# Sample attention with a plain f32 product, the two maps combined in one VectorE step, and the merge's panels split on ScalarE and VectorE

## The chip, the core and the metric

The kernel runs on one core of a Trainium2 chip. The core has TensorE (matrix products, PE in the profile, with PEld for the loading of its stationary operand), VectorE (DVE), ScalarE (ACT), GpSimd (POOL) and SyncE (SP, which here issues all DMA transfers). Each engine works through its own instructions in a fixed order; semaphores hold an instruction until what it needs is there. The metric is the time of one execution on the device in microseconds (us), as the median of several runs.

## The reference, cut to what matters

One layer of an encoder is applied to two sequences, a prompt of 512 tokens and a sample of 1024, each of width 1024. The part that the change touches is the attention, whose map is the difference of two softmax maps:

```python
def block(args):                                  # 128 queries at a time, 8 heads
    s = jnp.einsum('bqhmd,bkhmd->bhmqk', qblk, kf) * scale      # m: the two maps
    p = jax.nn.softmax(s + bias[None, :, None], axis=-1)
    a = p[:, :, 0] - lam * p[:, :, 1]
    return jnp.einsum('bhqk,bkhe->bqhe', a, vf)   # value width 128
...
g = jax.nn.sigmoid(gates)
merged = g[:, :, 0] * (att @ w_proj_attn) + g[:, :, 1] * (y_ssm @ w_proj_ssm)
return merged @ w_out
```

Before it stand an RMS norm and a large input projection, beside it a state-space branch (y_ssm), behind it a norm with a residual and a gated feed-forward network. All data are f32.

## The kernel before

Tiles have 128 partitions. For precision, nearly every product is made of three matmuls in the type f32r: an operand x is split into a high part (x rounded to f32r) and a low part (x minus the high part), and `gemm` (L162 to L167) adds high x high, high x low and low x high in one PSUM tile. `split` (L133) makes the two parts: "act_dve" with a ScalarE copy (L136) and a VectorE subtraction (L137), otherwise with two GpSimd steps (L142, L143). `split_panel` (L145) does this for a panel of 256 weight columns in two halves of 128 x 1024.

The stages, in the order of time: input norm; projections, with the prompt's attention laid between those of keys and queries; convolution, state-space scans and gates; then the sample's attention together with "side work" (32 blocks of gated products with 24 matmuls of 512 columns each: one pass of w_proj_attn for the prompt, three passes of w_proj_ssm); then the merge stage; then the feed-forward network.

The attention goes head by head (8), and in a head over query tiles of 128, in pairs (q2). For a query tile and each of the two maps it makes the scores (s, L291 and L292: four matmuls of 512 columns for 1024 keys), adds the bias and finds the minimum on VectorE (L294), and takes the exponential on ScalarE (L297). Then the maps are combined: VectorE does the first half of the keys in one step (L304), GpSimd the other half in two (L303, L306); VSH = 4 sets the halves. The combined map is transposed on TensorE in blocks of 128 (t, L310); ScalarE copies four blocks as the high part (L313) and VectorE makes the low part (L314). For a pair of query tiles the product with the values (o, out of `gemm`) takes three matmuls of 256 columns for each block of 128 keys. The values' two parts (vh, vl) are made on GpSimd. At the end of 512 queries a mean square (ms, L328) is made for the later norm.

The merge stage runs on 512-token chunks: `load_merged` for the prompt, then `out_proj` (panels of w_out, products of 256 columns), `merge` for each of the two sample chunks (panels of w_proj_attn, products of 512 columns, gated on VectorE), and `norms` (L1054 to L1077: norm, residual, second norm, transposes). The panels of `out_proj` and `merge` are split on GpSimd before the change.

The order of the instructions on each engine is set when the program is built: a scheduler of the framework simulates the program with costs of its own and lets each engine take what is ready, with the order of the code as the priority. So a change of what an engine has to do also changes where other instructions stand.

Of the kernel before, what the change touches and what calls it, by code (L numbers as in the profile page):

```python
# [18 lines left out]
P = 128  # L19
# [10 lines left out]
Q0, K0, V0, Z0, XBC0, DT0, G0 = 0, 1024, 2048, 3072, 4096, 5632, 5664  # L30
SEGK = 119
SKP = 2304
VSH = 4
PU = (1, 1)
OT = ("gt", 2)
NG = 2
# [42 lines left out]
def hybrid_trunk_kernel(ctx: ExitStack, tc: tile.TileContext, a: dict, y_prompt, y_sample):  # L79
# [48 lines left out]
    def staged(pool, shape, *srcs, tag="raw", bufs=None):  # L128
        raw = pool.tile(shape, F32, tag=tag, name=tag, bufs=bufs)
        for part, src in srcs:  # L130
            load(out=raw[part] if part is not None else raw, in_=src)
        return raw

    def split(hi, lo, raw, eng=None):
        if eng == "act_dve":
            S.copy(hi, raw)  # L136
            V.tensor_sub(lo, raw, f(hi))  # L137
        elif eng == "act_pool":
            S.copy(hi, raw)
            G.tensor_sub(lo, raw, f(hi))  # L140
        else:
            G.tensor_scalar(hi, raw, 1.0, 0.0, op0=ALU.mult, op1=ALU.add)  # L142
            G.tensor_sub(lo, raw, f(hi))  # L143
# [18 lines left out]
    def gemm(ps, pairs):  # L162
        n = len(pairs)
        for i, (ah, al, bh, bl) in enumerate(pairs):
            TE.matmul(ps, ah, bh, start=(i == 0), stop=False)  # L165
            TE.matmul(ps, ah, bl, start=False, stop=False)  # L166
            TE.matmul(ps, al, bh, start=False, stop=(i == n - 1))  # L167
# [96 lines left out]
    def attention(base, SL, h, got, pend, zq, msq, qk, pp, at, qr, s_ps, t_ps, o_ps):  # L264
        nkb = SL // P
        tb = got["tb"]
        qh, ql, km = zip(got[0], got[1])
        v_h = at.tile([P, nkb, P], F32R, tag="vh", name="vh", bufs=1)
        v_l = at.tile([P, nkb, P], F32R, tag="vl", name="vl", bufs=1)
        raw = staged(qr, [P, nkb, P], (None, v_d[base:base + SL, h * P:(h + 1) * P].rearrange("(b p) e -> p b e", p=P)))  # L270
        split(v_h[:], v_l[:], raw[:])
        for qc in range(SL // 512):
            ops = o_ps.tile([P, 512], F32, tag="o", name="o")
            for q2 in range(2):
                aT = [at.tile([P, 2, 4, 256], F32R, tag=f"aT{b0}", name="aT", bufs=2 - b0 // 4)
                      for b0 in range(0, nkb, 4)]
                for u in range(2):
                    if pend and (q2, u) == PU:
                        pend.pop()()
                    qt = qc * 4 + q2 * 2 + u  # L280
                    qs = slice(qt * P, (qt + 1) * P)
                    off = P * (nkb - 1 - qt)
                    nm = pp.tile([P, 2], F32, tag="nm", name="nm")
                    zs = pp.tile([P, 2], F32, tag="zs", name="zs")
                    z0 = zq[:, h, qt:qt + 1]
                    pm = []
                    for m in range(2):
                        sps = s_ps.tile([P, SL], F32, tag="s", name="s")
                        for kc in range(0, SL, 512):
                            ks = slice(kc, kc + 512)  # L290
                            TE.matmul(sps[:, ks], qh[m][:, qs], km[m][:, ks], start=True, stop=False)  # L291
                            TE.matmul(sps[:, ks], ql[m][:, qs], km[m][:, ks], start=False, stop=True)  # L292
                        pt = pp.tile([P, SL], F32, tag=f"p{m}", name="pt", bufs=3)
                        V.tensor_tensor_reduce(out=pt[:], in0=sps[:], in1=tb[:, off:off + SL], scale=-1.0,  # L294
                                               scalar=3.0e38, op0=ALU.add, op1=ALU.min,
                                               accum_out=nm[:, m:m + 1])
                        S.activation(out=pt, in_=pt, func=AF.Exp, bias=nm[:, m:m + 1], scale=-1.0,  # L297
                                     accum_out=(z0, zs[:, 0:1])[m])
                        pm.append(pt)
                    V.reciprocal(zs[:, 0:1], zs[:, 0:1])  # L300
                    V.scalar_tensor_tensor(zs[:, 1:2], zs[:, 0:1], z0, neglam, op0=ALU.mult, op1=ALU.mult)  # L301
                    ca, cb = slice(0, SL * VSH // 8), slice(SL * VSH // 8, SL)
                    G.tensor_scalar(pm[1][:, cb], pm[1][:, cb], zs[:, 1:2], 0.0, op0=ALU.mult, op1=ALU.add)  # L303
                    V.scalar_tensor_tensor(pm[0][:, ca], pm[1][:, ca], zs[:, 1:2], pm[0][:, ca],  # L304
                                           op0=ALU.mult, op1=ALU.add)
                    last_add.append(G.tensor_add(pm[0][:, cb], pm[0][:, cb], pm[1][:, cb]))  # L306
                    for b0 in range(0, nkb, 4):
                        ps = t_ps.tile([P, 4, P], F32, tag="t", name="t")
                        for j in range(4):
                            TE.transpose(ps[:, j, :], pm[0][:, (b0 + j) * P:(b0 + j + 1) * P], ident)  # L310
                        us = slice(u * P, (u + 1) * P)
                        ab = aT[b0 // 4]
                        S.copy(ab[:, 0, :, us], ps)  # L313
                        V.tensor_sub(ab[:, 1, :, us], ps, f(ab[:, 0, :, us]))  # L314
                    if u == 0:
                        yield
                gemm(ops[:, q2 * 256:q2 * 256 + 256],
                     [(v_h[:, b, :], v_l[:, b, :], aT[b // 4][:, 0, b % 4, :], aT[b // 4][:, 1, b % 4, :]) for b in range(nkb)])
                yield
            av = pp.tile([P, 512], F32, tag="av", name="av", bufs=1)  # L320
            S.copy(av, ops)
            store(out=att_d[h * P:(h + 1) * P, base + qc * 512:base + qc * 512 + 512], in_=av)

            def mean_square(av=av, qc=qc):
                S.activation(out=av, in_=av, func=AF.Square)
                ps = t_ps.tile([P, 4, P], F32, tag="t", name="ms")
                for j in range(4):
                    TE.matmul(ps[:, 0, j:j + 1], av[:, j * P:(j + 1) * P], onec, start=True, stop=True)  # L328
                V.tensor_copy(msq[:, h, qc * 4:qc * 4 + 4], ps[:, 0, 0:4])
            pend.append(mean_square)  # L330
# [538 lines left out]
    with ExitStack() as ph3:  # L869
# [22 lines left out]
        def merge(c, aTt):  # L892
            cs = slice(c * 512, (c + 1) * 512)
            hi, lo = big_pair()
            for p0 in range(0, D, 256):
                w = split_panel(a["w_proj_attn"][0][:, p0:p0 + 256], eng="pool")
                for b in range(2):
                    r0 = p0 + b * P
                    kb = r0 // P
                    gt = wk.tile([P, 512], F32, tag="gt", name="gt")  # L900
                    pt = wk.tile([P, 512], F32, tag="pt", name="pt", bufs=1)
                    load(out=gt, in_=g_d[r0:r0 + P, cs])
                    S.activation(out=gt, in_=gt, func=AF.Tanh, scale=0.5)
                    load(out=pt, in_=part_d[r0:r0 + P, cs])
                    ps = mm_tile(512)
                    gemm_fm(ps, w, slice(b * P, (b + 1) * P), aTt)
                    V.scalar_tensor_tensor(gt, gt, 1.0, ps, op0=ALU.add, op1=ALU.mult)
                    V.tensor_add(gt, gt, pt)
                    S.activation(out=hi[:, kb, :], in_=gt, func=AF.Copy, scale=0.5)
                    V.scalar_tensor_tensor(lo[:, kb, :], gt, 0.5, f(hi[:, kb, :]), op0=ALU.mult, op1=ALU.subtract)  # L910
            return hi, lo
# [120 lines left out]
        with ExitStack() as ph3a:  # L1032
# [4 lines left out]
            def out_proj(mT):  # L1037
                tiles = [mp.tile([P, D], F32, tag="mt", name="mt", bufs=4) for _ in range(4)]
                sums = wk.tile([P, 4, 4], F32, tag="ms4", name="ms4")
                for p0 in range(0, D, 256):  # L1040
                    w = split_panel(a["w_out"][0][:, p0:p0 + 256], eng="pool")
                    for j in range(4):
                        ps = mm_tile(256)
                        gemm_tm(ps, w, mT, slice(j * P, (j + 1) * P))
                        S.copy(tiles[j][:, p0:p0 + 256], ps)
                        sq = wk.tile([P, 256], F32, tag="gt", name="msq")
                        S.activation(out=sq, in_=ps, func=AF.Square, accum_out=sums[:, j, p0 // 256:p0 // 256 + 1])
                return tiles, sums
# [160 lines left out]
```

## Time and profile before

| what | us |
|---|---|
| median of three runs | 3239.67 |
| lowest and highest of them | 3237.82, 3248.19 |
| the profiled execution, and its span | 3245.1, 3243.3 |
| TensorE busy | 3049.5 (94%) |
| VectorE busy | 1842.6 (57%) |
| ScalarE busy | 1209.3 (37%) |
| GpSimd busy | 1034.0 (32%) |

The times come from runs on the device; everything on single engines comes from one profiled execution, whose span is what the engines' records cover. The page gives busy times by engine, the span in 40 slices, the chain of work that ended last, and groups of instructions by line with their mean. A TensorE that is busy is not at its peak, since a matmul's record holds its latency, and matmuls overlap. The trace behind the page can be asked for stretches, single instructions in order of time, and waits.

### The profile page before, as it was taken

To read this page: it belongs to the slowest core of one execution; us is meant where nothing else is said; L and a number is where in the kernel's file an instruction comes from. 1 tells how busy PE (TensorE), PEld (TensorE's weight loads), DVE (VectorE), ACT (ScalarE), POOL (GpSimd) and SP (SyncE) were. 2 spreads that over 40 slices of the span, in tenths; PEclk is the share of its full clock that TensorE was granted. 3 is DMA by queue.
4 is the path that set the end of the run, shared out by engine and by line. 5 is a ranking of instruction groups with operands and counts; after the bars stand their busy time and mean duration, and the time that the engine had idled before them with its cause. 6 is when DMAs were issued, how large, how long until landed. Compare 5 with 4: busy or idle time off the path is not lost.

```text
span 3243.3 us, 44646 instructions
## 1 busy us (share of the span) xinstructions
PE 3049.5 (94%) x16667; PEld 2677.0 (83%) x16667; DVE 1842.6 (57%) x2913; ACT 1209.3 (37%) x2255; POOL 1034.0 (32%) x796
## 2 busy tenths in 40 slices
PE   7999999999899999899999888878999899989998
PEld 7988887888787778687887777778999899978787
DVE  5114443455228994487788664776656766632444
ACT  4003333333113433466666523243333333322343
POOL 1003332000143442377567344433333433210100
PEclk9999999999999999999999998888999899999999
DMA  4623332223554454755555055544333333363354
GB/s 146 194 96 116 112 99 83 69 72 110 165 174 132 149 157 147 205 173 164 162 148 159 30 191 182 187 140 135 99 99 97 101 96 101 105 202 100 117 165 131
DMA packets 443325, 430.36 MB, mean 133 GB/s; under 512 B 25356, under 2 KB 360417, under 8 KB 442045
## 3 DMA queue, kind: packets, MB, share of 16 engines
q1 hardware_dynamic: 443109, 427.52, 42.8%
q8 instruction: 131, 2.15, 0.3%
q14 instruction: 85, 0.70, 0.1%
HBM read 315.37 MB, written 120.44 MB: 134 GB/s over the span
## 4 chain that ended last, share of the span: by engine, by line
PE 63%; DMA 12%; DVE 10%; issue 6%; POOL 4%; ACT 3%; SPq 1%; POOLq 0%; ACTq 0%; DVEq 0%
PE acc L165 9%; PE acc L167 9%; PE acc L166 9%; PE mm L165 5%; PE mm L167 5%; PE mm L166 5%; PE d L167 4%; PE d L166 3%; PE d L165 3%; DMA araw<-r_d 1%; DMA raw<-k_d 1%; DMA wraw<-in_w_gate_up_dram 1%; DMA gt<-g_d 1%; PE yd L772 1%; PE st_ps L675 1%
## 5 line engine op out<-in xcount | busy, mean ns | idle before, releaser
L165 PE MATMUL acc<-hT,whi 128*128 128x512 f32 x1056 | 420.9, 399 | 2.8 <-ACT st L435 2.8
L166 PE MATMUL acc<-hT,whi 128*128 128x512 f32 x1056 | 416.1, 394 | 0.0
L167 PE MATMUL acc<-hT,wlo 128*128 128x512 f32 x672 | 263.7, 392 | 0.0
L297 ACT ACTIVATE pt<-pt,nm 128x1024 f32<-128x1024 f32 (+1 forms) x192 | 193.3, 1008 | 125.5 <-DVE nm L294 115.3
L165 PEld LDWEIGHTS acc<-hT,whi 128*128 128x128 f32 x1056 | 198.5, 188 | 47.9 <-issue 5.5
L294 DVE CUSTOM_DVE_ANT_0 pt<-s,tb 128x1024 f32<-128x1024 f32 (+1 forms) x192 | 197.6, 1040 | 64.4 <-PE s L292 51.2
L166 PEld LDWEIGHTS acc<-hT,whi 128*128 128x128 f32 x1056 | 198.6, 188 | 42.2 <-issue 3.6
L165 PE MATMUL acc<-whi,hT 128*128 128x256 f32 x768 | 226.3, 295 | 0.1
L166 PE MATMUL acc<-wlo,hT 128*128 128x256 f32 x768 | 225.2, 293 | 0.0
L167 PE MATMUL acc<-whi,hT 128*128 128x256 f32 x768 | 224.2, 292 | 0.0
L167 PE MATMUL d<-dhi,fl 128*128 128x512 f32 x528 | 207.8, 394 | 8.3 <-DVE fl L137 8.3
L165 PE MATMUL d<-dhi,fh 128*128 128x512 f32 x528 | 207.7, 393 | 8.3 <-ACT fh L136 8.3
L166 PE MATMUL d<-dlo,fh 128*128 128x512 f32 x528 | 207.1, 392 | 0.0
L137 DVE TENSOR_TENSOR fl<-raw,fh 128x896 fp32r<-128x896 f32 (+1 forms) x72 | 85.9, 1195 | 200.4 <-ACT fh L136 200.4
L165 PE MATMUL mm<-op,wy 128*128 128x384 f32 x528 | 178.8, 339 | 10.3 <-ACT op L136 8.1
L167 PE MATMUL mm<-op,wy 128*128 128x384 f32 x528 | 178.7, 338 | 0.7 <-DVE wy L137 0.7
L166 PE MATMUL mm<-op,wy 128*128 128x384 f32 x528 | 178.3, 338 | 0.0
L303 POOL TENSOR_SCALAR pt<-pt,zs 128x512 f32<-128x512 f32 (+1 forms) x96 | 88.2, 919 | 255.4 <-DVE zs L301 213.5
L232 POOL TENSOR_TENSOR ql<-raw,qh 128x512 fp32r<-128x512 f32 x48 | 63.2, 1331 | 299.6 <-ACT qh L229 295.5
L165 PEld LDWEIGHTS acc<-whi,hT 128*128 128x128 f32 x768 | 148.6, 194 | 9.9 <-issue 8.5
L136 ACT CAST fh<-raw 128x896 fp32r<-128x896 f32 (+1 forms) x72 | 70.8, 983 | 227.7 <-PE d L166 212.7
L167 PE MATMUL acc<-hT,whi 128*128 128x512 f32 x384 | 155.5, 405 | 0.0
(358 smaller groups left out, 8612.6 us busy)
## 6 DMA issues: line engine op xcount, KB each, us to landing
wraw<-in_w_in_dram SPq DMA_DIRECT2D x60, 512.0 KB
wraw<-in_w_gate_up_dram SPq DMA_DIRECT2D x92, 256.0 KB
raw<-ff_d SPq DMA_DIRECT2D x48, 448.0 KB
wr<-in_w_gate_up_dram SPq DMA_DIRECT2D x80, 256.0 KB
ff_d<-c SPq DMA_DIRECT2D x88, 192.0 KB
g_d<-st SPq DMA_DIRECT2D x48, 256.0 KB
xg<-xs_d SPq DMA_DIRECT2D x48, 256.0 KB
gt<-g_d SPq DMA_DIRECT2D x48, 256.0 KB
```

What stands on the lines that cost most here:

```text
L136: S.copy(hi, raw)
L137: V.tensor_sub(lo, raw, f(hi))
L165: TE.matmul(ps, ah, bh, start=(i == 0), stop=False)
L166: TE.matmul(ps, ah, bl, start=False, stop=False)
L167: TE.matmul(ps, al, bh, start=False, stop=(i == n - 1))
L232: G.tensor_sub(q_l[:, s_], q_r[:, s_], f(q_h[:, s_]))
L294: V.tensor_tensor_reduce(out=pt[:], in0=sps[:], in1=tb[:, off:off + SL], scale=-1.0, scalar=3.0e38, op0=ALU.add, op1=ALU.min, accum_out=nm ...
L297: S.activation(out=pt, in_=pt, func=AF.Exp, bias=nm[:, m:m + 1], scale=-1.0, accum_out=(z0, zs[:, 0:1])[m])
L303: G.tensor_scalar(pm[1][:, cb], pm[1][:, cb], zs[:, 1:2], 0.0, op0=ALU.mult, op1=ALU.add)
L675: TE.matmul(ps, b_g, xw, start=True, stop=True)
L772: TE.matmul(yps[:, hs], ms[0][:, h, :], x_g[:, hs], start=True, stop=True)
```

## The change

In the sample's attention (`plain`, more than 512 keys) the product with the values is one f32 matmul for each block of 128 keys instead of three f32r matmuls: the values stay as loaded, without a split, and the transposed map is only copied, without a low part. In both attentions one VectorE step over all keys combines the two maps, and GpSimd has no part in it. The values have a tile of their own (vf, two buffers) instead of a buffer of the ring `raw`. The panels of `merge` and `out_proj` are split by ScalarE and VectorE.

```diff
-VSH = 4
...
-        v_h = at.tile([P, nkb, P], F32R, tag="vh", name="vh", bufs=1)
-        v_l = at.tile([P, nkb, P], F32R, tag="vl", name="vl", bufs=1)
-        raw = staged(qr, [P, nkb, P], (None, v_d[base:base + SL, h * P:(h + 1) * P].rearrange("(b p) e -> p b e", p=P)))
-        split(v_h[:], v_l[:], raw[:])
+        plain = SL > 512
+        v_f = at.tile([P, nkb, P], F32, tag="vf", name="vf", bufs=2)
+        load(out=v_f, in_=v_d[base:base + SL, h * P:(h + 1) * P].rearrange("(b p) e -> p b e", p=P))
+        if not plain:
+            v_h, v_l = [at.tile([P, nkb, P], F32R, tag=t_, name=t_, bufs=1) for t_ in ("vh", "vl")]
+            split(v_h[:], v_l[:], v_f[:])
...
-                aT = [at.tile([P, 2, 4, 256], F32R, tag=f"aT{b0}", name="aT", bufs=2 - b0 // 4)
-                      for b0 in range(0, nkb, 4)]
+                aT = [at.tile([P, 4, 256], F32, tag=f"aT{b0}", name="aT", bufs=2) if plain else
+                      at.tile([P, 2, 4, 256], F32R, tag="aT", name="aT", bufs=2) for b0 in range(0, nkb, 4)]
...
-                    ca, cb = slice(0, SL * VSH // 8), slice(SL * VSH // 8, SL)
-                    G.tensor_scalar(pm[1][:, cb], pm[1][:, cb], zs[:, 1:2], 0.0, op0=ALU.mult, op1=ALU.add)
-                    V.scalar_tensor_tensor(pm[0][:, ca], pm[1][:, ca], zs[:, 1:2], pm[0][:, ca],
-                                           op0=ALU.mult, op1=ALU.add)
-                    last_add.append(G.tensor_add(pm[0][:, cb], pm[0][:, cb], pm[1][:, cb]))
+                    last_add.append(V.scalar_tensor_tensor(pm[0], pm[1], zs[:, 1:2], pm[0], op0=ALU.mult, op1=ALU.add))
...
+                        if plain:
+                            S.copy(ab[:, :, us], ps)
+                            continue
...
-                gemm(ops[:, q2 * 256:q2 * 256 + 256],
-                     [(v_h[:, b, :], v_l[:, b, :], aT[b // 4][:, 0, b % 4, :], aT[b // 4][:, 1, b % 4, :]) for b in range(nkb)])
+                if plain:
+                    for b in range(nkb):
+                        TE.matmul(ops[:, q2 * 256:q2 * 256 + 256], v_f[:, b, :], aT[b // 4][:, b % 4, :],
+                                  start=b == 0, stop=b == nkb - 1)
+                else:
+                    gemm(ops[:, q2 * 256:q2 * 256 + 256],
+                         [(v_h[:, b, :], v_l[:, b, :], aT[0][:, 0, b, :], aT[0][:, 1, b, :]) for b in range(nkb)])
...
-                w = split_panel(a["w_proj_attn"][0][:, p0:p0 + 256], eng="pool")
+                w = split_panel(a["w_proj_attn"][0][:, p0:p0 + 256])
...
-                    w = split_panel(a["w_out"][0][:, p0:p0 + 256], eng="pool")
+                    w = split_panel(a["w_out"][0][:, p0:p0 + 256])
```

The lines of the changed kernel are numbered one less than before down to the attention, and four or five more behind it. TensorE in the sample's attention, before: the last side matmul of the whole stage (f), then scores (s), products (o) and transposes (t) by themselves.

```order
L167 MATMUL f<-yTt,whi 128x512
L291 MATMUL s<-km,qh 128x512
L292 MATMUL s<-km,ql 128x512
L291 MATMUL s<-km,qh 128x512
L292 MATMUL s<-km,ql 128x512
L291 MATMUL s<-km,qh 128x512
L292 MATMUL s<-km,ql 128x512
L291 MATMUL s<-km,qh 128x512
L292 MATMUL s<-km,ql 128x512
L165 MATMUL o<-aT,vh 128x256
L310 MATMUL t<-ident,pt 128x128 x4
L166 MATMUL o<-aT,vh 128x256
```

Some 14 query tiles follow behind these rows without any side matmul. TensorE now, near the end of the stage, in the last but one query tile:

```order
L319 MATMUL o<-aT,vf 128x256 x4
L307 MATMUL t<-ident,pt 128x128 x4
L293 MATMUL s<-km,ql 128x512
L292 MATMUL s<-km,qh 128x512
L293 MATMUL s<-km,ql 128x512
L292 MATMUL s<-km,qh 128x512
L293 MATMUL s<-km,ql 128x512
L165 MATMUL f<-yTt,whi 128x512
L166 MATMUL f<-yTt,whi 128x512
L307 MATMUL t<-ident,pt 128x128 x4
L164 MATMUL f<-yTt,whi 128x512
```

The product is one row for four blocks, and side matmuls stand between the attention's steps up to the end. VectorE in the merge stage, before, at the first norm (mt: its tiles, xr: the residual's input, gt and big: the gated products of a merge and their two parts, araw: the attention's rows as they are loaded):

```order
L1063 SCALAR_TENSOR_TENSOR mt<-mt,mr,pmw 128x512 x8
L1064 TENSOR_TENSOR mt<-mt,xr 128x512
L907 SCALAR_TENSOR_TENSOR gt<-gt,mm 128x512
L1064 TENSOR_TENSOR mt<-mt,xr 128x512
L907 SCALAR_TENSOR_TENSOR gt<-gt,mm 128x512
L908 TENSOR_TENSOR gt<-gt,pt 128x512
L1064 TENSOR_TENSOR mt<-mt,xr 128x512
L910 SCALAR_TENSOR_TENSOR big<-gt,big 128x512
L137 TENSOR_TENSOR big<-araw,big 128x512 x2
```

The same place now:

```order
L1068 SCALAR_TENSOR_TENSOR mt<-mt,mr,pmw 128x512 x8
L915 SCALAR_TENSOR_TENSOR big<-gt,big 128x512
L1069 TENSOR_TENSOR mt<-mt,xr 128x512
L136 TENSOR_TENSOR big<-araw,big 128x512
L1069 TENSOR_TENSOR mt<-mt,xr 128x512
L136 TENSOR_TENSOR big<-araw,big 128x512
L912 SCALAR_TENSOR_TENSOR gt<-gt,mm 128x512
L136 TENSOR_TENSOR wlo<-wraw,whi 128x1024 x2
L913 TENSOR_TENSOR gt<-gt,pt 128x512
L359 SCALAR_TENSOR_TENSOR araw<-araw,cols 128x512
```

The low parts of a panel (wlo) now stand in VectorE's order between the norm's and the merge's steps.

## Rows read from the trace of the kernel before

**Rows 1.** Busy time in stretches: from:to, then length, busy us by engine, clock, DMA.

```profile
200.00:545.00 345.00, 345.00 (x1694) 288.66 (x1693) 139.39 (x323) 110.18 (x226) 108.83 (x116) 1.00 0.34 107
1311.50:1420.00 108.50, 95.30 (x463) 77.78 (x462) 62.71 (x98) 59.79 (x88) 52.93 (x38) 0.97 0.69 189
1420.00:1740.00 320.00, 308.48 (x1719) 261.57 (x1718) 249.61 (x406) 204.16 (x327) 211.89 (x150) 0.99 0.54 161
1740.00:1839.00 99.00, 87.61 (x552) 73.48 (x550) 84.53 (x158) 65.32 (x115) 61.28 (x50) 0.98 0.27 88
1839.00:2212.00 373.00, 299.97 (x1822) 270.43 (x1823) 239.12 (x329) 125.67 (x325) 156.73 (x87) 0.89 0.51 164
1905.00:1976.00 71.00, 47.90 (x201) 38.18 (x200) 64.24 (x77) 18.06 (x37) 39.01 (x20) 0.84 0.63 210
```

**Rows 2.** Timeline of TensorE: start us, length us, line, operands, form, count.

```profile
859.90 1.02 PE L697 MATMUL yo_ps<-state,ct 128*128 128x512 f32 x2
...
1499.87 0.40 PE L165 MATMUL f<-yTt,whi 128*128 128x512 f32 x1
...
1504.07 0.39 PE L165 MATMUL f<-yTt,whi 128*128 128x512 f32 x1
...
1511.12 0.28 PE L166 MATMUL o<-aT,vh 128*128 128x256 f32 x1
...
1512.32 0.29 PE L167 MATMUL o<-aT,vl 128*128 128x256 f32 x1
...
1523.46 1.03 PE L310 MATMUL t<-ident,pt 128*128 128x128 f32 x8
```

**Rows 3.** The f32 matmul's records by tile: ns min/median/max, first and last start.

```profile
L697 PE MATMUL yo_ps<-state,ct x40: 592/592/1090, 859.9 to 952.2; 128*128 128x512 f32 x40
```

**Rows 4.** Groups on TensorE from 1740 to 1839 us: count, busy us, mean ns.

```profile
L291 PE MATMUL s<-km,qh 128*128 128x512 f32 x62 | 27.1, 436 | 6.1 <-DVE nm L294 5.9
...
L165 PE MATMUL o<-aT,vh 128*128 128x256 f32 x80 | 24.2, 302 | 2.1 <-ACT aT L313 1.7 <-POOL vl L143 0.3
...
L310 PE MATMUL t<-ident,pt 128*128 128x128 f32 x148 | 21.8, 274 | 2.2 <-DVE aT L314 2.0
```

**Rows 5.** Groups of the attention's steps on VectorE, whole span.

```profile
L314 DVE TENSOR_TENSOR aT<-t,aT 128x512 fp32r<-128x512 f32 x160 | 107.9, 684 | 43.0 <-ACT aT L313 42.6
...
L304 DVE SCALAR_TENSOR_TENSOR pt<-pt,zs 128x512 f32<-128x512 f32 x64 | 67.1, 1048 | 1.5
```

**Rows 6.** Groups of the panels' two steps on GpSimd, on ScalarE and VectorE.

```profile
L143 POOL TENSOR_TENSOR wlo<-wraw,whi 128x1024 fp32r<-128x1024 f32 x44 | 114.5, 2618 | 1.0
...
L136 ACT CAST whi<-wraw 128x1024 fp32r<-128x1024 f32 x72 | 73.6, 1049 | 204.5 <-PE acc L167 100.0 <-PE acc L166 83.7 <-PE f L167 9.7
...
L142 POOL TENSOR_SCALAR whi<-wraw 128x1024 fp32r<-128x1024 f32 x60 | 69.1, 1157 | 269.9 <-PE mm L167 62.4 <-PE acc L167 60.5 <-DMA wraw<-in_w_out_dram 49.8
...
L137 DVE TENSOR_TENSOR wlo<-wraw,whi 128x1024 fp32r<-128x1024 f32 x40 | 48.2, 1239 | 76.4 <-ACT whi L136 67.1 <-PE dt_ps L587 9.3
```

**Rows 7.** Waits from 1839 to 2212 us: total us, times, longest us.

```profile
PE tr_ps L1075 <- DVE mt L1071: 19.4, 7, 8.5
...
PE mm L167 <- POOL wlo L143: 13.1, 5, 6.6
```

**Rows 8.** Timeline of VectorE and GpSimd in the first merge.

```profile
1909.57 10.37 DVE L1063 SCALAR_TENSOR_TENSOR mt<-mt,mr,pmw 128x512 f32<-128x512 f32 x8
...
1912.52 5.55 POOL L143 TENSOR_TENSOR wlo<-wraw,whi 128x1024 fp32r<-128x1024 f32 x2
```

**Rows 9.** The norm's groups, and the same by tile: ns min/median/max, first and last start.

```profile
L1063 DVE SCALAR_TENSOR_TENSOR mt<-mt,mr,pmw 128x512 f32<-128x512 f32 x24 | 29.8, 1310 | 0.2
...
L1064 DVE TENSOR_TENSOR mt<-mt,xr 128x512 f32<-128x512 f32 x24 | 24.4, 1025 | 9.1 <-DMA xr<-in_x_sample_dram 9.1
...
L1063 DVE SCALAR_TENSOR_TENSOR mt<-mt,mr,pmw x24: 737/750/2882, 1909.6 to 2167.3; 128x512 f32<-128x512 f32 x24
L1064 DVE TENSOR_TENSOR mt<-mt,xr x24: 675/684/2893, 1919.9 to 2190.8; 128x512 f32<-128x512 f32 x24
```

## The prediction

> **What bounds the kernel now.** I read the stretches first (busy time of each engine, granted clock), then single starts on TensorE, then the waits. The prompt's attention is no place for a gain: from 200 to 545 us TensorE is busy for all of 345 us at clock 1.00 [rows 1], the projections cover everything else there, and the change leaves TensorE's work in it alone. Two stages remain. The sample's attention with its side work runs from 1311.5 to 1839 us, 527.5 us in three stretches: a head of 108.5, a middle of 320 in which TensorE is busy for 308.5, and a tail of 99 without side work, in which VectorE is the busiest for its part (84.5 of 99) and TensorE has 87.6 [rows 1]. Then comes the stage with the three out-projections and two merges, 1839 to 2212 us, 373 us, with TensorE busy for 300 at clock 0.89, VectorE 239, GpSimd 157, ScalarE 126 [rows 1].
>
> A busy share flatters TensorE, because a matmul's 0.3 to 0.4 us is mostly latency. So I price work by the distance of starts. Two starts of the side matmul (f, 512 columns) lie 1504.07 - 1499.87 = 4.20 us apart with 18 steps, 0.233 us each; ten steps of the product with the values (o, 256 columns) take 1.20 us, 0.120 each; eight transposes take 1.03 us in all, 0.108 each without the last one's own 0.27 [rows 2, 4]. The small records of the mean square (ms) are counted like transposes. From the code the stage has 768 f, 512 score matmuls (also 512 columns) and some 50 gate matmuls, 512 transposes, 768 o and 128 records of ms: 1330 x 0.233 + 640 x 0.108 + 768 x 0.120 = 471 us of the 527.5. So TensorE is close to the bound, with 56 us lost. Of these the tail alone loses 21: it has 62 score matmuls of each of two lines, 80 products of each of three, 148 transposes [rows 4] and 40 ms records, 28.9 + 28.8 + 16.0 + 4.3 = 78 us of work in 99.
>
> **The change part by part: the product.** One f32r triple of a 128-key block is 3 x 0.120 = 0.360 us. The f32 matmul stands in the trace with 512 columns: two records, together 1.02 us [rows 2], of which a record's own length is 0.59 [rows 3], so the second starts 0.43 us after the first, 0.86 us for one matmul. Half the columns are at least 0.43 us. The upper bound takes each 256-column record as dear as the f32r matmul with 512 columns, 2 x 0.233 = 0.467 [rows 2]. No f32 matmul of 256 columns is in the trace, so I take 0.45, midway. 256 such products instead of 768 matmuls cost TensorE 256 x 0.09 = +23 us (+18 to +27): this edit makes the bounding engine's work longer, from 471 to 494 us.
>
> The Trainium skill (FP8 and Floating Point Precision, TensorE Precision Notes) says the same against it: true FP32 takes four passes through the array. If each pass cost what an f32r matmul of 256 columns costs here, the product would be 0.48 us and the sum +31 us; the f32 row above is cheaper than that, so I keep the row.
>
> **What it takes off the other engines.** VectorE loses the low part of the transposed maps, 0.684 us [rows 5] twice for each of 64 query tiles, 87.6 us. Its combination grows from 512 elements at 1.05 us [rows 5] to 1024; the nearest 1024-wide step with two operands in SBUF takes 1.24 us [rows 6], so +12 us. The sum of VectorE in the three stretches falls from 397 us [rows 1] to about 322. GpSimd loses both combination steps and the split of the values. ScalarE keeps its copies.
>
> What is that worth? Only what TensorE lost by waiting for them, the 56 us, and of these the head's idle 13 (108.5 - 95.3 [rows 1]) belongs to loads and stays. The new order speaks for a gain: before, the last side matmul stands some 14 query tiles ahead of the end, now it stands in the last two, so the tail, where VectorE held TensorE up, gets filler. Counting the other 43 us of loss halved, the stage is 494 + 13 + 22 = 529 us, +2. Bounds: -19 if nearly all the waits go (489 + 13 + 6 = 508) and +27 if the waits stay as they are under the dearest product. I take 0, as 322 of 527 us on VectorE leaves it no stretch in which it is the bound. The first two loads of the values now stand ahead of the second map's queries in the DMA queue; 20 more side matmuls stand in front of the scores there and cover 20 x 0.233 = 4.7 us of it; without that cover it would add to the head.
>
> **The panels.** Forty half panels (16 in the two merges, 24 in the three out-projections) go from GpSimd, 1.16 + 2.62 us, to ScalarE and VectorE, 1.05 + 1.24 us [rows 6]. Gone are TensorE's waits for GpSimd, 13.1 us [rows 7]. Added are 42 us on ScalarE, with 126 of 373 busy [rows 1] no bound, and 40 x 1.24 = 50 us on VectorE, which matters: from 1905 to 1976 us it is busy for 64 of 71 [rows 1], and TensorE waits for its normalised tiles, 19.4 us in the stage [rows 7]. In that stretch ten of the forty new steps stand in its order, 12.4 us. Behind them wait the eight additions of the residual, the merge's results and so the transposes.
>
> Against this stands what the trace shows of VectorE beside GpSimd. Eight steps of the norm took 10.4 us there, while GpSimd's two subtractions ran from 1912.5 to 1918.1 [rows 8]; in the whole stage the step's mean is 1.31 and its median 0.75, and the residual's 1.03 and 0.68 [rows 9]. These two lines alone lose 24 x 0.56 + 24 x 0.34 = 22 us; the merge's two lines with two SBUF operands and the loads of the attention show the same pattern, so I count 40 for all, with 22 as the lower end. The Trainium skill (SBUF — State Buffer, Who interferes with whom) has a rule for it: a VectorE instruction with two SBUF inputs and a GpSimd instruction that reads SBUF exclude one another for the whole instruction. By that rule nearly all of the lengthening goes with the panels, and the trace agrees: the longest norm step, 2.88 us [rows 9], is no longer than one GpSimd subtraction (2.62 us [rows 6]) and its own 0.74.
>
> So VectorE's account in the stage is +50 - 40 = +10, in effect neutral where it is the bound, and TensorE's waits for the panels go: -13. Besides, the panel is ready after 2.3 rather than 3.8 us, and some of the stage's low clock goes with the waits: -3. The stage: **-16 us**, bounds -30 (VectorE's relief also shortens the 19 us of waits for the norm) and +12 (below).
>
> **Sum.** 0 - 16 = -16 us, that is 3229 us of time against the profiled run's 3245.1 (span 3243.3). This run lies 5.4 us above the median of the runs, 3239.67; the same difference from the median is 3224 us.
>
> **The rivals.** (1) TensorE pays the product in full: the waits in the attention were not VectorE's, and the products cost 0.467. Then the attention gets 12 us longer (+27, less 15 for the filled tail), and with -14 from the panels the result is 3238. For it speaks that TensorE already has 471 of 527 us; against it the tail. (2) The waits vanish: -19 in the attention and -28 in the merge stage, 3193. VectorE's and GpSimd's relief speak for it, the added 23 us against it. (3) Slower: the panels are caught in VectorE's in-order queue. A panel's low part now stands behind eight norm steps and behind loads that it does not need, and TensorE waits for it as it waited for GpSimd. If the lengthened steps don't get shorter, 50 us are added, half of them (25) in the stretches where VectorE is the bound; less the 13, +12, with +2 in the attention: 3254. It decides from the point at which the relief is under half of the 50. (4) The side work keeps TensorE as it was and the panels were covered anyway: 3240.
>
> **How the numbers follow.** About 0.3%, 9.7 us, is what a measurement here can tell from no change. The forecast (-8 to -30) has 0.42, of which 0.38 is beyond 9.7; rival 1 has 0.22, rival 2 0.15, rival 3 0.14, rival 4 0.07. Faster: 0.38 + 0.15 = 0.53. Slower: rival 3 and a little of rival 4, 0.16. Same: 0.31. The range leaves out the far half of rivals 2 and 3: 3198 to 3254.
>
> **What would show it.** After the change: products of two records each, about 0.45 us a block; TensorE busy through the last 100 us of the attention and that stage within 10 us of 527; the norm step's mean near 0.75; no wait for GpSimd in the merges, and that stage near 357 us. I am wrong if a product's distance is above 0.47, if VectorE's steps in the merges stay above 1.1 us, or if TensorE waits there for the panels' low parts from VectorE.

## The result and the profile after

The changed kernel takes 3215.68 us (median of four runs, 3210.19 to 3217.31), the kernel before 3242.39 beside it: a ratio of 0.9914 with a 95% interval of 0.9892 to 0.9935. In a later set of five runs it was 3219.78 against 3247.39, 0.9906 (0.9893 to 0.9920). So it is faster by 27 us; 16 were predicted. The total came out close, but not by the working: the merge stage gave 40 us where 16 were forecast, and the attention took 11 where 0 was. The changed kernel's profile also starts the attention 8 us later and is 7 us shorter behind the merge stage, which makes up its 28 us.

The stretches of the changed kernel, in the columns of [rows 1] (from:to, length, busy us of PE, PEld, DVE, ACT, POOL with their counts, granted clock, DMA share, GB/s): head, middle and tail of the sample's attention, then the merge stage.

```profile
1319.50:1430.00 110.50, 93.63 (x398) 74.93 (x397) 53.62 (x79) 54.71 (x81) 26.22 (x21) 0.91 0.66 190
1430.00:1745.00 315.00, 299.13 (x1506) 247.71 (x1505) 214.04 (x331) 207.75 (x335) 99.51 (x64) 0.99 0.50 147
1745.00:1858.00 113.00, 111.22 (x564) 93.62 (x562) 73.12 (x125) 68.26 (x116) 0.00 (x0) 0.98 0.33 107
1858.00:2192.00 334.00, 284.29 (x1822) 261.30 (x1823) 209.73 (x365) 161.43 (x361) 24.90 (x15) 0.93 0.56 186
```

The tail is full now: TensorE is busy for 111.2 of 113 us, where it was busy for 87.6 of 99 [rows 1]. The head and the middle together are only 3 us shorter than before (425.5 against 428.5), although side work has moved from them to the tail. In the last row VectorE is busy for 29 us less than before although 44 us of panels were added to it, GpSimd has almost nothing, and the clock is 0.93 instead of 0.89.

TensorE's timeline in the middle, the new product beside transposes and scores (start us, length us, operands, count, idle before):

```profile
1519.18 3.72 PE L319 MATMUL o<-aT,vf 128*128 128x256 f32 x16 [0.24 <-ACT aT L311]
```

Sixteen records for eight blocks: two for each product. The last record's own length is 0.379, so two starts lie (3.72 - 0.379) / 15 = 0.223 us apart, and a product costs 0.445 us.

The attention's combination on VectorE, then the norm's two lines in the merge stage, by tile (ns min/median/max, first and last start) and as groups with the panels' low part among them (count, busy us, mean ns):

```profile
L303 DVE SCALAR_TENSOR_TENSOR pt<-pt,zs 128x1024 f32<-128x1024 f32 x64 | 91.5, 1429 | 2.1
```

```profile
L1068 DVE SCALAR_TENSOR_TENSOR mt<-mt,mr,pmw x24: 747/748/1793, 1928.3 to 2146.6; 128x512 f32<-128x512 f32 x24
L1069 DVE TENSOR_TENSOR mt<-mt,xr x24: 679/690/1284, 1934.2 to 2168.7; 128x512 f32<-128x512 f32 x24
```

```profile
L136 DVE TENSOR_TENSOR wlo<-wraw,whi 128x1024 fp32r<-128x1024 f32 x36 | 43.1, 1222 | 32.2 <-ACT whi L135 32.2
...
L1068 DVE SCALAR_TENSOR_TENSOR mt<-mt,mr,pmw 128x512 f32<-128x512 f32 x24 | 18.3, 835 | 0.1
L1069 DVE TENSOR_TENSOR mt<-mt,xr 128x512 f32<-128x512 f32 x24 | 17.0, 713 | 5.0 <-DMA xr<-in_x_sample_dram 4.3 <-DMA xr<-in_x_prompt_dram 0.6
```

The norm's step went from a mean of 1310 to 835 ns with the same median, the residual's from 1025 to 713 [rows 9]: what vanished are the long ones among them.

What TensorE waits for in that stage (total us, times, longest us):

```profile
PE mm L164 <- ACT whi L135: 18.1, 2, 15.3
PE tr_ps L1080 <- DVE mt L1076: 8.1, 2, 7.7
PE ms L333 <- ACT av L330: 6.6, 1, 6.6
```

The wait for GpSimd's low parts (13.1 us in [rows 7]) is gone, the wait for the normalised tiles fell from 19.4 to 8.1. The longest one left, for ScalarE's whi, stands where the feed-forward network begins, and the kernel before has it too (14.8 us).

**Where the time went.** From the first side matmul to the last product with the values, and from there to the last transpose of the norms. Idle is the length less TensorE's busy time; the second stage has the same 1821 or 1822 matmuls in each kernel.

| kernel | attention | PE busy | PE idle | DVE busy | merge stage | PE busy | PE idle |
|---|---|---|---|---|---|---|---|
| before | 512.6 | 479.7 | 32.9 | 393.1 | 371.0 | 299.7 | 71.3 |
| changed | 523.8 | 493.3 | 30.5 | 338.1 | 331.2 | 284.1 | 47.1 |
| changed, second profile | 521.9 | 490.2 | 31.7 | 338.3 | 329.8 | 285.4 | 44.4 |
| product alone | 518.1 | 491.5 | 26.6 | 322.9 | 377.9 | 300.1 | 77.8 |
| combination alone | 523.7 | 483.3 | 40.4 | 412.6 | 367.7 | 295.9 | 71.8 |
| panels alone | 509.7 | 481.9 | 27.8 | 394.4 | 327.2 | 286.9 | 40.3 |
| panels alone, second profile | 510.8 | 478.5 | 32.3 | 396.5 | 331.2 | 284.8 | 46.4 |
| combination and panels | 530.7 | 482.8 | 47.9 | 412.8 | 330.5 | 286.6 | 43.9 |
| product and panels | 512.1 | 488.8 | 23.3 | 324.9 | 336.6 | 289.2 | 47.4 |

Ahead of the attention the profiles differ by up to 16 us (it starts at 1326 us in the kernel before and at 1328 to 1342 in the others). Kernels with nothing changed up to there start late too, so the change's own start, 8 us later, isn't laid to it. Behind the merge stage the two profiles of the panels alone differ by 5 us, so the 7 us there aren't laid to it either. With the attention unchanged its length was 505.7 to 514.0 us in five profiles. Differences under some 8 us in the attention's length therefore decide nothing.

### The profile page after: what moved, and what is told of

The parts are those of the page before. It is cut to its first block, busy times and chain, and to the rows that moved or that the text cites. A ratio compares the mean times of both kernels' runs of the same rounds, so it can differ in the third digit from the quotient of the medians.

```text
span 3215.5 us, 43466 instructions
## 1 busy us (share of the span) xinstructions
PE 3051.8 (95%) x16411; PEld 2676.9 (83%) x16411; DVE 1771.6 (55%) x2825; ACT 1246.6 (39%) x2295; POOL 657.4 (20%) x508
## 5 line engine op out<-in xcount | busy, mean ns | idle before, releaser
L135 ACT CAST whi<-wraw 128x1024 fp32r<-128x1024 f32 (+1 forms) x115 | 115.9, 1036 | 232.6 <-PE acc L166 99.1
```

## The experiments

**One part at a time.** Each undoes two of the three parts, or one.

The product alone, as an edit of the changed kernel (the combination is halved between VectorE and GpSimd, the panels are on GpSimd):

```diff
-    last_add.append(V.scalar_tensor_tensor(pm[0], pm[1], zs[:, 1:2], pm[0], op0=ALU.mult, op1=ALU.add))
+    ca, cb = slice(0, SL * VSH // 8), slice(SL * VSH // 8, SL)
+    G.tensor_scalar(pm[1][:, cb], pm[1][:, cb], zs[:, 1:2], 0.0, op0=ALU.mult, op1=ALU.add)
...
-    w = split_panel(a["w_out"][0][:, p0:p0 + 256])
+    w = split_panel(a["w_out"][0][:, p0:p0 + 256], eng="pool")
```

> Only the f32 product: the maps are still combined by VectorE and GpSimd in halves, and the panels of the merges and out-projections stay on GpSimd. Theory A (the product costs TensorE 256 x 0.085 = 22 us, the panels give the gain): the attention, from the first side matmul to the last product, 512 us before, becomes 520 to 535, the merge stage (last product to last transpose, 371 us before) stays within 8 us, and the whole is slower by 5 to 22 us. Rival B (what VectorE is spared in the attention carries a part of the gain): the attention gets no longer than 515 and the whole is no slower or faster.

Measured: 3261.44 us against 3246.56, 1.0050 (1.0035 to 1.0065), slower by 15 us, as theory A has it; the attention, 518.2 us, lies between the two theories' ranges. The tail of its attention:

```profile
1746.00:1846.00 100.00, 99.76 (x511) 84.45 (x510) 57.21 (x103) 57.69 (x97) 49.42 (x36) 0.99 0.29 89
```

TensorE has no gap left, and VectorE is idle for 43 us. So filling the tail works, but what it saves is used up by the dearer product. Of the 15 us the stage table shows 5.5 in the attention and 7 in the merge stage, each within what profiles of one code differ by.

The combination alone, as an edit of the kernel before:

```diff
-                    ca, cb = slice(0, SL * VSH // 8), slice(SL * VSH // 8, SL)
-                    G.tensor_scalar(pm[1][:, cb], pm[1][:, cb], zs[:, 1:2], 0.0, op0=ALU.mult, op1=ALU.add)
-                    V.scalar_tensor_tensor(pm[0][:, ca], pm[1][:, ca], zs[:, 1:2], pm[0][:, ca],
-                                           op0=ALU.mult, op1=ALU.add)
-                    last_add.append(G.tensor_add(pm[0][:, cb], pm[0][:, cb], pm[1][:, cb]))
+                    last_add.append(V.scalar_tensor_tensor(pm[0], pm[1], zs[:, 1:2], pm[0], op0=ALU.mult, op1=ALU.add))
```

> Only the combination of the two maps in one VectorE step; product and panels as before. Theory A: TensorE's work is the same and the attention is near its bound, so within 8 us of before in the attention, nothing in the merge stage; the whole -8 to +8 us. Rival B: GpSimd's two steps (2.4 us a query tile) held up the chain and VectorE; the attention gets shorter by 10 to 25 us.

Measured: 3256.81 us, 1.0031 (1.0018 to 1.0043), slower by 10 us, and the attention is 11 us longer: outside the ranges of both theories. The tail, 110 us where it was 99, with VectorE at 96.0 (84.5 before, [rows 1]), and the step in it:

```profile
1747.00:1857.00 110.00, 97.93 (x602) 84.20 (x600) 95.99 (x172) 73.00 (x127) 27.59 (x16) 0.94 0.28 83
```

```profile
L302 DVE SCALAR_TENSOR_TENSOR pt<-pt,zs 128x1024 f32<-128x1024 f32 x18 | 24.9, 1384 | 0.0
```

VectorE gains 11.5 us of work there and the tail gets 11 us longer.

The panels alone, as an edit of the kernel before (the two calls of `split_panel` as in the change, nothing else):

```diff
-    w = split_panel(a["w_proj_attn"][0][:, p0:p0 + 256], eng="pool")
+    w = split_panel(a["w_proj_attn"][0][:, p0:p0 + 256])
...
-    w = split_panel(a["w_out"][0][:, p0:p0 + 256], eng="pool")
+    w = split_panel(a["w_out"][0][:, p0:p0 + 256])
```

> Only the panels of the merges and out-projections on ScalarE and VectorE; attention as before. Theory A: the merge stage falls from 371 us to 331 to 340, the attention stays at 512 within 5 us, and the whole is 30 to 42 us faster, more than the full change. Rival B: the merge stage falls by 10 to 20 us only, since a part of its gain came from the side work that no longer ends early.

Measured: 3208.69 us, 0.9879 (0.9861 to 0.9897), 38 us faster. Theory A holds, with the merge stage 4 us below its range. More than the whole gain of the change is here, and the merge stage has it (327 us, 44 less than before; 331 in a second profile).

Combination and panels, with the product in three f32r matmuls:

> Combination and panels as changed, the product again with three f32r matmuls. Theory A: the merge stage as in the changed kernel (331 to 340 us), the attention 500 to 512 us, the whole 35 to 55 us faster than before and so faster than the full change. Rival B: without the f32 product VectorE keeps the low parts and the tail has no side work, so the attention is as long as in the full change (523) or longer and the whole no faster than the full change.

Measured: 3216.58 us, 0.9911 (0.9893 to 0.9929). Rival B holds: the attention is longer than in the changed kernel (530.7 us), and the total is no better (0.9914 there). So on top of the long combination the product costs nothing. That it takes VectorE from 413 to 338 us there would explain it, but isn't shown to be the reason. The profiled execution is the longest of the four here, 5 us above their median.

**Product and panels**, with the combination as before:

> The product in f32 and the panels, with the combination as before (VectorE and GpSimd a half each). Theory A, the product costs what it cost alone (attention +5.5 us, about +16 us in all) because TensorE is the busy engine of the attention (99.8 of the 100 us of the tail with the product alone): attention 514 to 521 us, in all 3213 to 3226 us. Theory B, the product's cost stands or falls with the panels too: 3200 to 3210 us, attention under 510 us.

Measured: 3218.19 us against 3247.39, 0.9906 (0.9891 to 0.9921). In time theory A holds: 12 us above the panels alone of the same set. By the stages it doesn't: the attention is 512.1 us, near its length with the panels alone, with 10 us more of TensorE's work and 9 us less idle time. The two profiled executions lie 9.7 us apart: 5.8 ahead of the attention, 1.3 in it, 5.4 in the merge stage and -2.8 behind that. So the product's 12 us are plain in the time, and where they arise is open. The same set has all three parts at 3219.78 us, so by time the long combination adds next to nothing to product and panels.

**Does TensorE set the attention's pace?** The changed kernel with one f32r matmul of a block in place of the f32 one, which leaves out the low parts of values and maps:

```diff
+    v_h = at.tile([P, nkb, P], F32R, tag="vr", name="vr", bufs=1)
+    S.copy(v_h[:], v_f[:])
...
-    TE.matmul(ops[:, q2 * 256:q2 * 256 + 256], v_f[:, b, :], aT[b // 4][:, b % 4, :],
+    TE.matmul(ops[:, q2 * 256:q2 * 256 + 256], v_h[:, b, :], aT[b // 4][:, b % 4, :],
```

> The changed kernel with the product with the values as one f32r matmul of a block instead of one f32 matmul; it leaves out the low parts, and so precision. That takes 0.445 - 0.12 = 0.325 us of TensorE from each of the attention's blocks, 83 us in all, and nothing from the other engines. Theory A, TensorE sets the attention's pace: attention 523 to 445..470 us, in all 3135 to 3165 us. Theory B, VectorE (341 us of 523) and the order of its steps set it: attention 495 to 515 us, in all 3187 to 3208 us.

Measured: 3147.28 us, 0.9691 (0.9675 to 0.9707), where the changed kernel has 0.9914: some 70 us less. The attention is 459.8 us, and theory A holds. Of 83 us taken from TensorE 64 come back in the stage: TensorE sets its pace, with VectorE nearly unchanged at 341 us.

**Other divisions of the combination**, on the kernel with the panels alone. A quarter on VectorE:

```diff
-VSH = 4
+VSH = 2
```

> As the kernel with the panels alone, but VectorE takes a quarter of each combination of the maps and GpSimd three quarters (a half each before). Theory A, VectorE is what is late in the attention's tail (87 of 102 us busy) and each step taken off it counts: some 0.3 us of VectorE for each of 64 tiles less, attention 509 to 498..505 us, in all 3196 to 3206 us. Theory B, GpSimd's longer chain (half as much again on some 2.5 us) and its use of the port that VectorE shares eat it: attention 508 to 520 us, in all 3208 to 3220 us.

Measured: 3226.39 us, 0.9936 (0.9921 to 0.9951). Both steps on GpSimd, in the attention's tail of 133 us:

```profile
L306 POOL TENSOR_TENSOR pt<-pt 128x768 f32<-128x768 f32 x21 | 38.8, 1851 | 1.3
...
L304 DVE SCALAR_TENSOR_TENSOR pt<-pt,zs 128x256 f32<-128x256 f32 x20 | 23.1, 1156 | 0.1
...
L303 POOL TENSOR_SCALAR pt<-pt,zs 128x768 f32<-128x768 f32 x21 | 21.2, 1010 | 38.4 <-DVE zs L301 28.7 <-DVE zs L300 5.0 <-ACT aT L313 2.4
```

VectorE's step is half as wide as before and not shorter (1156 ns, 1048 in [rows 5]): it runs beside GpSimd's. Theory B holds in kind, but the loss is beyond its ranges: 3226 us against 3208 to 3220, an attention of 537 us against 508 to 520. Five eighths:

```diff
-VSH = 4
+VSH = 5
```

> As the kernel with the panels alone, with five eighths of each combination on VectorE and three eighths on GpSimd (a half each in the kernel before; a quarter on VectorE gave a tail of 133 us and an attention of 537 us, all of it on VectorE a tail of 109 us and 530 us). Theory A, each tile waits for GpSimd's two steps one after the other, so that a smaller part for it still helps: attention 500 to 507 us, in all 3198 to 3206 us. Theory B, the half is the best division, since VectorE is the later engine in the tail (87 of 102 us): attention 509 to 520 us, in all 3208 to 3220 us.

Measured: 3207.66 us, 0.9871 (0.9858 to 0.9885), the same time as the half in the same set (3206.37). Yet neither theory's range for the attention holds: in the profile it is 522.7 us long, 12 more than with the half, and starts 8 us earlier. By time the two divisions can't be told apart.

**Why the panels gain so much.** Two attempts to give GpSimd its work back without letting TensorE wait for it. First the low part alone on GpSimd:

```diff
-    w = split_panel(a["w_out"][0][:, p0:p0 + 256])
+    w = split_panel(a["w_out"][0][:, p0:p0 + 256], eng="act_pool")
```

> As the kernel with the panels alone, but of the merge stage's panels ScalarE makes the high part and GpSimd the low part. GpSimd keeps the tensor_sub of about 2.6 us of the 3.8 us that it spent on a half panel, VectorE gets no panel work. Theory A (port contention): about two thirds of the 44 us of the merge stage are lost again, stage 350 to 362 us, in all 3230 to 3243 us. Theory B (panels sooner): a half panel costs 2.6 us of GpSimd instead of 3.8, most of TensorE's waits for it go, stage 330 to 342 us, in all 3211 to 3223 us.

Measured: 3221.37 us, 0.9924 (0.9909 to 0.9938). The merge stage, what TensorE waits for in it, and two of VectorE's steps:

```profile
1839.80:2185.60 345.80, 291.16 (x1821) 265.60 (x1821) 211.43 (x328) 158.17 (x358) 111.47 (x50) 0.91 0.55 175
```

```profile
PE tr_ps L1075 <- DVE mt L1071: 22.7, 4, 8.2
...
PE mm L167 <- POOL wlo L140: 6.0, 4, 2.2
```

```profile
L1064 DVE TENSOR_TENSOR mt<-mt,xr 128x512 f32<-128x512 f32 x24 | 22.3, 930 | 8.8 <-DMA xr<-in_x_sample_dram 6.6 <-DMA xr<-in_x_prompt_dram 2.2
...
L354 DVE SCALAR_TENSOR_TENSOR araw<-araw,cols 128x512 f32<-128x512 f32 x16 | 17.2, 1076 | 30.2 <-DMA araw<-r_d 30.2
```

VectorE has no panels here and is still busy for 211 us: the steps that take 209.5 - 44 = 165.5 us in the changed kernel take 211. TensorE's wait for the normalised tiles is back (22.7 us), the wait for GpSimd's panels is small (6.0). The stage lies 15 to 19 us above that of the panels alone, where the wait for the normalised tiles is 6.6 and 8.1 us. So 15 to 19 of the 40 us hang on the low parts being made on GpSimd. VectorE's slowed steps have the larger share in them, as the longer wait for the normalised tiles shows; the waits for GpSimd itself are in that figure too. The stage lies between the two theories' ranges, the time inside B's: neither cause alone explains the 40.

Then GpSimd reading finished panels into a tile that nobody reads:

```diff
+            if scr is not None:
+                for k in range(s.start, s.stop):
+                    for c0 in (0, 128):
+                        ph, pl = f(hi[:, k, c0:c0 + 128]), f(lo[:, k, c0:c0 + 128])
+                        G.tensor_scalar(scr, ph, 1.0, 0.0, op0=ALU.mult, op1=ALU.add)
+                        G.tensor_sub(scr, ph, pl)
...
-                w = split_panel(a["w_proj_attn"][0][:, p0:p0 + 256], eng="pool")
+                w = split_panel(a["w_proj_attn"][0][:, p0:p0 + 256], scr=scr)
```

> The panels' split as in the kernel with the panels alone (3208.7 us, merge stage 327 us against 371 before), but GpSimd reads each finished half panel of the merge stage again, in pieces of 128 columns (a tensor_scalar and a tensor_sub for each), into a scratch tile that nobody reads; no panel waits for it, so TensorE can't wait for GpSimd. Theory A, the gain came mostly from VectorE's steps getting shorter when GpSimd is quiet (L1063 1310 to about 800 ns): with GpSimd busy again VectorE's steps are long again and the merge stage goes back to 345 to 365 us, in all 3225 to 3245 us. Theory B, the gain came from the panels being there sooner: the merge stage stays at 327 to 335 us, in all 3207 to 3217 us, although VectorE's steps are long again.

Measured: 3290.47 us, 1.0139 (1.0116 to 1.0161), the merge stage 417 us, outside both ranges. What held up the work:

```profile
PE mm L171 <- ACT whi L136: 75.2, 15, 10.2
...
ACT whi L136 <- POOL scr L159: 65.0, 16, 7.9
```

A panel's buffer can't be filled again before GpSimd has read it, so TensorE waited for GpSimd by another way. The run doesn't separate the theories. The same without holding the buffer wasn't tried.

**The changed kernel beside the panels alone**, five rounds:

> The changed kernel again, beside the other three of this call on the same chip. 3216 us within some 4 us.

> The panels alone, again, beside the changed kernel. Theory A, the product and the combination together cost some 7 us on top of the panels: 3205 to 3212 us, 5 to 10 us under the changed kernel. Theory B, the 7 us were chance between calls: within 3 us of it.

Measured: 0.9906 (0.9893 to 0.9920) for the changed kernel and 0.9870 (0.9856 to 0.9883) for the panels alone, 3219.78 against 3206.37. The intervals don't meet, and the 13 us between them are more than theory A's 5 to 10. The panels alone beat both kernels.

## Why the prediction was right and wrong

**Right: the product's price.** 0.445 us a block was measured and 0.45 taken. The Trainium skill (FP8 and Floating Point Precision, TensorE Precision Notes) lets a true FP32 product make four passes, by the f32r matmul's distance an estimate of 0.48; the trace has two records and 0.445, and the measurement stands. That TensorE is the stage's bound is right too, by the one-pass run.

**Wrong in size: the attention, 0 forecast, +11 and +9 measured in two profiles.** The step that failed is "counting the other 43 us of loss halved". The product added 256 x (0.445 - 0.360) = 22 us, as taken; with the stage 11 us longer, only 11 us of loss came back where 21 were counted. The tail did as the step says, TensorE's idle time there fell from 11.4 to 1.8 us. But in the head it rose from 13.2 to 16.9 and in the middle from 11.5 to 15.9 (rows above against [rows 1]), so of the idle time little went: 2.4 us in the stage, while busy time rose by 13.6.

In the middle the idle time goes with the long combination. From 100 us behind the first side matmul to 100 us ahead of the last product TensorE is idle for 14 to 21 us in the five profiles of kernels with one VectorE step, and for 9 to 13 in the seven with halves. The changed kernel and product and panels:

```profile
1434.10:1757.90 323.80, 308.36 (x1535) 255.30 (x1536) 221.50 (x345) 209.87 (x341) 95.41 (x61) 0.98 0.50 145
```

```profile
1441.70:1753.80 312.10, 302.01 (x1522) 251.77 (x1521) 207.21 (x339) 207.40 (x337) 196.89 (x147) 0.99 0.52 153
```

The combination was sized at 1.24 us and took 1.43, and its price was put down as hidden because VectorE is far from full (338 of 524 us). Alone it wasn't hidden: it cost 10 us. It stands in each tile's chain from scores to transposes, though TensorE's wait for it by name is only 1.2 us in the changed kernel. The times don't lay the whole miss on it either. Each of the two parts costs something on top of the panels in its own set, the product 12 us and the combination some 8, and both together 13. How the 11 us divide between them is open. Rival 1's attention (+12) came true in size, but with products at 0.445 and not at its 0.467.

The head has a wait that goes with the product, for the gate step on VectorE. TensorE's waits for that step in the attention (total us, times, longest us) in the kernel before, in the changed one, and in product and panels:

```profile
PE f L165 <- DVE gt L822: 1.6, 2, 0.9
```

```profile
PE f L164 <- DVE gt L827: 12.4, 6, 8.9
```

```profile
PE f L165 <- DVE gt L832: 10.1, 3, 8.9
```

In all four profiles with the f32 product there is one such wait of 8.9 to 10.0 us; in the nine with three f32r matmuls none is above 1.5. The kernel before has a wait of 6.2 us for GpSimd's km near that place instead, so the head as a whole loses only 4 us more. The values' loads stand in front of others in the DMA queue, as the prediction named; whether they cause the wait isn't shown, since the run that moves them wasn't made.

SyncE's queue at the head of the attention, in the changed kernel (start us, length us):

```profile
1338.27 6.86 SPq L269 DMA_DIRECT2D vf<-v_d  x2
...
1347.42 1.98 SPq L130 DMA_DIRECT2D raw<-q_d  x2
```

The second map's queries are issued 1347.42 - 1335.30 = 12.1 us after the first map's, in the kernel before 1338.18 - 1328.60 = 9.6 us: 2.5 us later.

**Right in kind, much too small: the merge stage, -16 forecast (bounds -30 and +12), -40 measured, outside the bounds.** Three terms. "TensorE's waits for the panels go, -13" came true. "VectorE +50 - 40 = +10" is mis-sized: 36 of the panels' steps fall in the stage, 44 us, and VectorE's sum still falls from 238.9 to 209.5, so the other steps lost 73 us, not 40. I had priced two lines by their means and guessed at the rest. Four more lines of 16 steps each lost 7 or 8 us apiece; two of them and one that reads PSUM, before and after (groups: count, busy us, mean ns):

```profile
L354 DVE SCALAR_TENSOR_TENSOR araw<-araw,cols 128x512 f32<-128x512 f32 x16 | 19.0, 1186 | 31.7 <-DMA araw<-r_d 31.7
...
L908 DVE TENSOR_TENSOR gt<-gt,pt 128x512 f32<-128x512 f32 x16 | 17.9, 1117 | 0.2
L907 DVE SCALAR_TENSOR_TENSOR gt<-gt,mm 128x512 f32<-128x512 f32 x16 | 10.9, 679 | 5.1 <-ACT gt L903 5.1
```

```profile
L359 DVE SCALAR_TENSOR_TENSOR araw<-araw,cols 128x512 f32<-128x512 f32 x16 | 12.0, 751 | 25.2 <-DMA araw<-r_d 25.2
...
L913 DVE TENSOR_TENSOR gt<-gt,pt 128x512 f32<-128x512 f32 x16 | 11.0, 690 | 7.9 <-DMA pt<-part_d 7.9
...
L912 DVE SCALAR_TENSOR_TENSOR gt<-gt,mm 128x512 f32<-128x512 f32 x16 | 11.0, 686 | 3.9 <-ACT gt L908 3.4 <-PE mm L166 0.5
```

The step that takes the product from PSUM (mm) was never long; those with both operands in SBUF fell by more than a third. TensorE's wait for the normalised tiles, for which the sum had nothing, went from 19.4 to 8.1. "Some of the low clock, -3" is the other mis-sized term. The same 1821 matmuls are busy for 299.7 us before and 284.1 after, 15.6 less, as the granted clock rises from 0.89 to 0.93. Before and after, one line of the merge's 512-column products (count, busy us, mean ns):

```profile
L167 PE MATMUL mm<-big,wlo 128*128 128x512 f32 x128 | 52.8, 413 | 13.1 <-POOL wlo L143 13.1
```

```profile
L166 PE MATMUL mm<-big,wlo 128*128 128x512 f32 x128 | 50.0, 391 | 1.8 <-DVE wlo L136 1.8
```

What a wait does to the matmuls behind it is plainest at the 8.9 us in the changed kernel's attention:

```profile
1352.98 0.39 PE L165 MATMUL f<-aTt,whi 128*128 128x512 f32 x1
1353.21 0.39 PE L166 MATMUL f<-aTt,whi 128*128 128x512 f32 x1
1362.46 0.80 PE L164 MATMUL f<-aTt,whi 128*128 128x512 f32 x1 [8.86 <-DVE gt L827]
1363.05 0.63 PE L165 MATMUL f<-aTt,whi 128*128 128x512 f32 x1
1363.48 0.63 PE L166 MATMUL f<-aTt,whi 128*128 128x512 f32 x1
```

Two starts lie 0.23 us apart ahead of the wait and 0.43 behind it; the granted clock is 1.00 from 1345 to 1353 us and 0.50 from 1362.5 to 1368, the levels of 2.4 and 1.2 GHz. Such a stretch of waiting is paid twice: once idle, and once in slower matmuls behind it. So -40 is -24 of idle time and -16 of busy time for the same matmuls.

The Trainium skill's rule (SBUF — State Buffer, Who interferes with whom) that VectorE with two SBUF operands and a GpSimd instruction that reads SBUF exclude one another agrees with most of what was measured: without GpSimd's panels the norm's step is at 835 ns, and with its subtractions alone the residual's addition is at 930, against 713 in the changed kernel; the norm's own step, at 860 there, is hardly slowed. Taken to the end the rule would have said that nearly all of the slow-down goes, that is the 73 us and not 40.

**Total.** The miss of 11 in the attention and of 24 in the merge stage went opposite ways, and 3224 came out 8 us high: that it is so close is luck. Rival 3 (the panels caught in VectorE's queue) was wrong: TensorE waits 2.4 us in all for a panel's low part from VectorE.

## What to carry to other kernels

Before GpSimd is given work beside VectorE, look at the spread between mean and median of VectorE's steps in that stretch, and add it up over all lines: here two lines showed 22 us and VectorE got 73 back. Where a step lies in the chain from scores to product, its length can count even if its engine is not full over the stage (the combination alone cost 10 us with VectorE busy for 413 of 524), so taking a helper out of it needs a run by itself. A change of three parts with one good one is worth taking apart: here the panels alone are 13 us better than all three together.

## What the hardware showed that I had not expected

The norm's step where GpSimd reads finished panels in pieces of 128 columns (ns min/median/max):

```profile
L1070 DVE SCALAR_TENSOR_TENSOR mt<-mt,mr,pmw x24: 771/944/1803, 1925.0 to 2224.7; 128x512 f32<-128x512 f32 x24
```

One f32 matmul of 256 columns is two records of 0.223 us, 3.7 times the f32r matmul's 0.120. With GpSimd busy for 320 of 417 us in pieces of 128 columns, VectorE's norm step had a median of 944 ns against 747 in the second profile of the panels alone, but a longest of only 1803; in the kernel before, GpSimd busy for 155 us in pieces of 1024 columns leaves the median at 750 and makes the longest 2882 [rows 9]. So beside the long GpSimd instructions a few steps were very long, and beside the short ones many were slightly long. The two runs also differ in how long GpSimd was busy, so the width alone isn't shown to be the reason.
